# Attention by half-head tiles with the v transposes behind the first scores; an opening with latent x first and stationary conditioning weights

## The chip, the cores and the metric

One core of one Trainium2 chip. Its engines work side by side, each on its own queue in order: TensorE (PE; PEld is its weight load), VectorE (DVE), ScalarE (ACT), GpSimd (POOL) and SyncE (SP, which here issues most DMAs). The metric is the device time of one execution in microseconds; lower is better.

## The reference

Two layers over 512 latent and 256 context tokens of width 1024. Cut to what matters here:

```python
mod_lat = silu(c) @ ada_w[l] + ada_b[l]          # 6 x 1024 columns: shift, scale, gate, twice
mod_ctx = silu(c_ctx) @ ada_w[l] + ada_b[l]
h_lat = rmsnorm(x, norm1_g[l]) * (1 + sc1) + sh1
h_ctx = rmsnorm(ctx, norm1_g[l]) * (1 + csc1) + csh1
z = h @ w_in[l]                                  # branches A, B (q, k, v), C and gates
# branch B, for each of 8 heads, two halves a of 64 columns:
s = einsum('qad,kad->aqk', q, k) * 64 ** -0.5    # q and k normalised and rotated before
p = softmax(s)
out = (p[0] - lam * p[1]) @ v                    # latent queries see all 768 keys, context queries 256
```

Behind it stand the merge of the three branches, `w_out`, a residual, a second modulated norm and a gated feed-forward with a width-3 convolution. In layer 1 only keys and values of the context are wanted.

## The kernel before, in words

Activations lie with features on the 128 partitions and tokens along the row. Products that must be accurate are done in three passes: each operand is split into a rounded high part (`hh`, `whi`; a cast on ACT) and a low part (`hl`, `wlo`; a subtraction on DVE), and high x high, low x high and high x low are added up in PSUM (`gemm`, L183 to L186). Weights come through `Stream`: raw tiles of 512 KB (`wraw`), two deep, cast by `split_to` and finished by `low`.

The order of every instruction is the order in which Python emits it. `weave` mixes generators: each yields an estimated cost, and the one that is least far along in its own total goes next. So the costs that are yielded, and the totals given beside them, are what sets the order on each engine.

The opening (`startup`, L413) loads x by feature tiles of all 768 tokens, and the conditioning weights in chunks of 512 columns, through one SP queue. The vector silu(c), silu(c_ctx) is the stationary operand of two columns, a raw weight row of 512 the moving one (`ada_pe`, L209, in plain fp32); a copy and four small transposes turn the row into columns. One chunk goes over DVE (`ada_dve`, L233). The squares of x are added up, a matmul with ones (L335) gives the sum per token, an inverse root follows in small DVE steps (`rsqrt_ops`), and a matmul (L349) spreads it over the partitions. Then x is normalised and modulated tile by tile (`norm_apply`, L360), and `step` (in `halves`) multiplies each ready tile with the first three weights of branch C.

Attention runs over the eight heads. While the scores and softmax of head h go on (`attn`), the projections of head h + 1 are woven in (`project`: products of 256 columns, L647 to L649, in pieces of 12; then v). Between two heads stands a turn (`turn`, L1333): `qk_tr` transposes rotated q and k in three token pieces and splits them into high and low parts. The tile `qk` holds for each half a of the head high and low parts in different partitions, `qw` the same for q with the two swapped, by DMA. A product of branch C (`c_fill`) fills PE meanwhile. `v_tr` then transposes and splits v. `attn` goes block by block over 128 queries: `scores` (L825) does the matmuls into PSUM (two buffers), a row minimum on DVE (`mn`), an exponential on ACT (`pa`); `combine` subtracts the two halves; `to_at` transposes the result and splits it (`ah`, `al`); `av` multiplies with v.

Of the kernel before, what the change touches and what calls it, by code (L numbers as in the profile page):

```python
# [11 lines left out]
F32 = mybir.dt.float32  # L12
# [117 lines left out]
class Net:  # L130
# [78 lines left out]
    def ada_pe(self, l, n):  # L209
        nc = self.nc  # L210
        ps = self.ad.tile([128, 512], F32, tag="ad", name="ad")
        for q in range(8):
            if q % 2 == 0:
                two = self.ast.take("k", l, n, q // 2)
            raw = two[:, q % 2 * 512:q % 2 * 512 + 512]
            nc.tensor.matmul(ps[0:2, :], lhsT=self.silu[:, q, :], rhs=raw, start=(q == 0), stop=(q == 7))
            if q % 2:
                self.ast.load_to(len(self.ast.keys) + self.ast.bufs)
            if q < 7:
                yield 1000  # L220
        rows = self.small.tile([2, 512], F32, tag="adarow", bufs=1, name="adarow")
        nc.scalar.copy(rows, ps[0:2, :])
        yield 1000

        def fin():
            pt = self.ad.tile([128, 512], F32, tag="ad", name="ad")
            for i in range(4):
                nc.tensor.transpose(pt[:, 2 * i:2 * i + 2], rows[:, i * 128:(i + 1) * 128], self.ident[0:2, 0:2])
            pv = pt[:, 0:8].rearrange("p (i s) -> p s i", s=2)
            self.ada_fin([pv[:, s, :] for s in range(2)], l, n)  # L230
        yield fin

    def ada_dve(self, l, n):  # L233
        nc = self.nc
        ns = 2 if l == 0 or n < 4 else 1
        acc = [self.ast.pool.tile([128, 512], F32, tag=f"aacc{s}", bufs=2, name="aacc") for s in range(ns)]
        for q in range(8):
            if q % 2 == 0:
                two = self.ast.take("k", l, n, q // 2)
            raw = two[:, q % 2 * 512:q % 2 * 512 + 512]  # L240
            for s in range(ns):
                sc = self.silu[:, q, s:s + 1]
                if q == 0:
                    nc.vector.tensor_scalar(acc[s], raw, sc, None, ALU.mult)
                else:
                    nc.vector.scalar_tensor_tensor(acc[s], raw, sc, acc[s], ALU.mult, ALU.add)
            if q % 2:
                self.ast.load_to(len(self.ast.keys) + self.ast.bufs)
            yield 1000

        def fin():
            pt = self.ad.tile([128, 512], F32, tag="ad", name="ad")
            for s in range(ns):
                for i in range(4):
                    nc.tensor.matmul(pt[:, 4 * s + i:4 * s + i + 1], lhsT=acc[s][:, i * 128:(i + 1) * 128],
                                     rhs=self.ones[:, 0:1], start=True, stop=True)
            self.ada_fin([pt[:, 4 * s:4 * s + 4] for s in range(ns)], l, n)
        yield fin
# [101 lines left out]
    def norm_apply(self, tmp, sc, xs, rb, seg, cut=8, pre=False):  # L360
# [52 lines left out]
    def startup(self, xp, xt, load_x, pkeys, evac):  # L413
        nc = self.nc
        pa, pb = self.parts()
        self.ast.start(xp, 2, 7, nc.sync)
        for n in (1, 1, 2, 1, 2, 1):
            for _ in range(n):
                load_x()
            self.ast.load_to(self.ast.loaded + (len(xt) > 1))  # L420
        self.ws.late = True
        rb = xp.tile([128, T], F32, tag="rb", bufs=1, name="rb")
        ada = self.ada_chunks(self.ada_pe, [(0, 2), (0, 0)])
        g3, g1 = (self.ada_chunks(f, [(0, n)]) for f, n in ((self.ada_dve, 3), (self.ada_pe, 1)))

        def two(*gs):
            for g in gs:
                next(g)
                next(g)

        k = 0
        for i in range(16):
            next(ada)
            if i == 2:
                self.ws.load_to(2)
            while k < 8 and i >= (1, 2, 4, 6, 8, 9, 10, 11)[k]:
                for o, m, _ in (pa, pb):
                    self.sq_acc(xp, k, xt[k][:, o:o + m], o, m)
                k += 1
            if i == 12:  # L440
                r = self.norm_stat(0, T)
            if i == 14:
                self.ws.split_to(1)
                self.ast.limit += 8
                self.ast.load_to(11)
                self.ws.load_to(3)
        self.ws.low()
        self.ws.split_to(2)
        self.norm_rows(rb[:, 0:512], r, 512)
        sc = self.scales(0, 0)  # L450
        self.scales_set(sc, 0, 0, 0, 4)
        self.norm_h()
        step, finish = self.halves(pkeys, self.segs, evac)
        tmp = lambda: xp.tile([128, T], F32, tag="nsq", bufs=2, name="nt")
        ga, gb = (self.norm_apply(tmp, sc, [x[:, o:o + m] for x in xt], rb[:, o:o + m], (o, m, s), 4, s == 0)
                  for o, m, s in (pa, pb))
        next(ga)
        for _ in ada:
            pass
        self.norm_rows(rb[:, 512:768], r[:, 4:6], 256)  # L460
        self.ast.load_to(15)
        for k in range(4):
            next(ga)
            if k in (0, 3):
                self.ws.low()
            step(k, pa, 0)
            if k:
                step(k - 1, pa, 1)
            if k == 1:
                self.ws.split_to(3)  # L470
        step(3, pa, 1)
        two(g3)
        two(g1)
        for k in range(4):
# [3 lines left out]
            if k:  # L478
                two(g3)
                if k == 3:  # L480
                    for _ in g3:
                        pass
                two(g1)
        step(0, pa, 2)
        step(1, pa, 2)
        for _ in g1:
            pass
        step(2, pa, 2)
        step(3, pa, 2)
        self.scales_set(sc, 0, 0, 4, 8)  # L490
        next(ga)
        for k in range(4, 8):
            step(k, pa, 0)
            step(k, pa, 1)
            next(ga if k < 7 else gb)
        for k in range(4, 8):
            if k < 7:
                next(gb)
            step(k, pa, 2)
# [1044 lines left out]
```

## Time and profile before

| | |
|---|---|
| median of three runs | 2684.49 us (2683.94 to 2686.37) |
| profiled execution | 2683.64 us, its span 2681.9 us |
| PE busy | 2611.5 us (97%) |
| DVE busy | 1660.8 us (62%) |
| ACT busy | 1011.5 us (38%) |
| POOL busy | 220.6 us (8%) |
| bytes moved | 254.33 MB, 95 GB/s over the span |

The span runs from the first to the last instruction; all times inside it count from its start. Busy shares hold for the whole span, while each stage has its own limit: the opening up to about 76 us, attention of layer 0 to about 556, of layer 1 from about 1600 to 2000, and between and after them merge and feed-forward. Matmuls are pipelined and their ends are modelled, so the distance between the starts of two of them is the cost of one, not the duration that the row shows.

### The profile page before, as it was taken

Reading aid. Unit: us, or ns where it says so; the run is one execution under the profiler, and the core shown is the slowest. Engines: PE = TensorE matmul, PEld = TensorE weight load, DVE = VectorE, ACT = ScalarE, POOL = GpSimd, SP = SyncE. Lnnn points to the kernel's source line nnn. Section 1 sums busy time; section 2 is a strip of 40 time slices with the busy share of each in tenths; the row PEclk is TensorE's granted clock in tenths of the full one; section 3 lists DMA queues with packets and bytes.
Section 4 is the critical chain, followed back from the end, with each engine's and each line's share of the span. In section 5 each row is a group of like instructions: output and inputs, shape, how many; then the busy total and the mean of one; then the engine's idle time right before and its main releaser. Section 6 shows DMA issues by size and latency. Waiting matters only on the chain.

```text
span 2681.9 us, 36899 instructions
## 1 busy us (share of the span) xinstructions
PE 2611.5 (97%) x14952; PEld 2254.3 (84%) x14952; DVE 1660.8 (62%) x2895; ACT 1011.5 (38%) x1711; POOL 220.6 (8%) x202
## 2 busy tenths in 40 slices
PE   8999999999999999999999999999999999999999
PEld 3889989888888888888888878888878888888887
DVE  5677877756556437544544567877867554654444
ACT  3455455442122224312322334554553232342432
POOL 0000000001111110100100100000001122020101
PEclk8999999999999999999999999999999999999999
DMA  5211221224233331222222232212125545233333
GB/s 224 81 44 58 57 69 48 58 73 146 96 126 105 108 134 63 79 79 79 79 79 79 85 104 67 67 51 65 56 69 171 175 164 180 71 95 102 94 103 110
DMA packets 79658, 254.33 MB, mean 95 GB/s; under 512 B 9200, under 2 KB 19712, under 8 KB 79104
## 3 DMA queue, kind: packets, MB, share of 16 engines
q1 hardware_dynamic: 64512, 196.64, 22.8%
q0 software_dynamic: 14544, 55.07, 6.4%
q8 instruction: 118, 1.93, 0.3%
q14 instruction: 52, 0.43, 0.0%
q10 hardware_dynamic: 432, 0.27, 0.0%
HBM read 234.63 MB, written 6.82 MB: 90 GB/s over the span
## 4 chain that ended last, share of the span: by engine, by line
PE 78%; DVE 14%; ACT 5%; issue 2%; DMA 1%; DVEq 0%; POOL 0%; SPq 0%; ACTq 0%; POOLq 0%
PE mm L183 22%; PE mm L186 21%; PE mm L184 21%; DVE wlo L69 3%; PE S L838 2%; ACT pa L847 2%; PE mm L647 2%; PE mm L648 2%; PE mm L649 2%; DVE qk L727 2%; ACT whi L83 1%; PE mmT L871 1%; DVE mn L845 1%; ACT qk L726 1%; DVE zs L697 1%
## 5 line engine op out<-in xcount | busy, mean ns | idle before, releaser
L183 PE MATMUL mm<-hh,whi 128*128 128x512 f32 (+1 forms) x2392 | 854.5, 357 | 11.9 <-ACT hh L376 9.8
L184 PE MATMUL mm<-hl,whi 128*128 128x512 f32 (+1 forms) x2392 | 819.1, 353 | 4.4 <-DVE hl L379 4.1
L186 PE MATMUL mm<-hh,wlo 128*128 128x512 f32 (+1 forms) x2392 | 752.2, 353 | 1.3 <-DVE wlo L69 1.3
L183 PEld LDWEIGHTS mm<-hh,whi 128*128 128x128 f32 x2392 | 452.2, 189 | 104.7 <-ACT hh L376 13.3
L184 PEld LDWEIGHTS mm<-hl,whi 128*128 128x128 f32 x2392 | 452.4, 189 | 69.0 <-DVE hl L379 9.3
L69 DVE TENSOR_TENSOR wlo<-wraw,whi 128x1024 fp32r<-128x1024 f32 x320 | 399.4, 1249 | 179.2 <-ACT whi L83 177.5
L186 PEld LDWEIGHTS mm<-hh,wlo 128*128 128x128 f32 x2392 | 414.3, 190 | 41.5 <-DVE wlo L69 3.5
L83 ACT CAST whi<-wraw 128x1024 fp32r<-128x1024 f32 x320 | 334.6, 1047 | 291.7 <-PE mm L184 250.1
L996 DVE SCALAR_TENSOR_TENSOR cv<-mm,pc,cv 128x511 f32<-128x511 f32 (+1 forms) x132 | 86.8, 658 | 181.8 <-ACT cv L995 180.9
L183 PE MATMUL mm<-ah,whi 128*128 128x512 f32 (+1 forms) x528 | 187.9, 356 | 0.0
L847 ACT ACTIVATE pa<-S,mn 128x768 f32<-128x768 f32 (+1 forms) x160 | 129.3, 813 | 150.1 <-DVE mn L845 122.6
L647 PE MATMUL mm<-whi,hh 128*128 128x256 f32 x640 | 183.3, 286 | 1.3 <-DVE cp L775 0.8
L648 PE MATMUL mm<-wlo,hh 128*128 128x256 f32 x640 | 181.1, 283 | 0.8 <-DVE wlo L69 0.8
L649 PE MATMUL mm<-whi,hl 128*128 128x256 f32 x640 | 180.9, 283 | 0.0
L184 PE MATMUL mm<-al,whi 128*128 128x512 f32 (+1 forms) x528 | 179.9, 354 | 0.0
L186 PE MATMUL mm<-ah,wlo 128*128 128x512 f32 (+1 forms) x528 | 161.7, 355 | 0.0
L995 ACT ACTIVATE cv<-mm,pc 128x512 f32<-128x512 f32 (+1 forms) x132 | 88.7, 705 | 177.2 <-PE mm L186 177.2
L1157 DVE SCALAR_TENSOR_TENSOR x<-mm,mod,x 128x512 f32<-128x512 f32 (+1 forms) x91 | 58.2, 659 | 138.7 <-PE mm L186 138.7
L1200 POOL TENSOR_TENSOR cv<-cv 128x768 f32<-128x768 f32 (+1 forms) x44 | 91.5, 2080 | 605.2 <-DVE cv L998 420.7
L647 PEld LDWEIGHTS mm<-whi,hh 128*128 128x128 f32 x640 | 121.7, 190 | 4.2 <-ACT cp L773 1.0
L648 PEld LDWEIGHTS mm<-wlo,hh 128*128 128x128 f32 x640 | 122.0, 191 | 1.3 <-DVE wlo L69 1.2
L649 PEld LDWEIGHTS mm<-whi,hl 128*128 128x128 f32 x640 | 121.9, 190 | 0.0
(232 smaller groups left out, 4028.4 us busy)
## 6 DMA issues: line engine op xcount, KB each, us to landing
wraw<-w SPq DMA_DIRECT2D x320, 512.0 KB, 3.6
araw<-ada POOLq DMA_DIRECT2D x80, 512.0 KB, 4.0
qw<-qk SPq DMA_DIRECT2D x80, 128.0 KB, 2.5
araw<-ada SPq DMA_DIRECT2D x16, 512.0 KB, 7.4
x<-xT SPq DMA_DIRECT2D x8, 384.0 KB, 6.1
srow<-sscr POOLq DMA_DIRECT2D x3, 1024.0 KB, 5.4
x<-xT POOLq DMA_DIRECT2D x8, 384.0 KB, 5.9
xscr<-x SPq DMA_DIRECT2D x8, 256.0 KB, 3.9
```

The source lines that it names most:

```text
L69: self.lo_eng.tensor_tensor(lo, raw, hi.bitcast(F32), ALU.subtract)
L83: self.nc.scalar.copy(hi, raw)
L183: nc.tensor.matmul(ps[:, :m], lhsT=hh, rhs=xh[:, o:o + m], start=st, stop=False)
L184: nc.tensor.matmul(ps[:, :m], lhsT=hh, rhs=xl[:, o:o + m], start=False, stop=False)
L186: nc.tensor.matmul(ps[:, :m], lhsT=hl, rhs=xh[:, o:o + m], start=False, stop=sp)
L647: nc.tensor.matmul(ps[:, :256], lhsT=hh[:, sl], rhs=hi[:, c:c + 256], start=(k == 0), stop=False)
L648: nc.tensor.matmul(ps[:, :256], lhsT=hh[:, sl], rhs=lo[:, c:c + 256], start=False, stop=False)
L649: nc.tensor.matmul(ps[:, :256], lhsT=hl[:, sl], rhs=hi[:, c:c + 256], start=False, stop=(k == 7))
L847: nc.scalar.activation(pa[:, :nk], ss[a], AF.Exp, bias=mn[:, a:a + 1], scale=-1.0, accum_out=sm[a])
L995: nc.scalar.activation(dst[:, o:o + m], s, AF.Identity, scale=w[1], bias=bias)
L996: nc.vector.scalar_tensor_tensor(dst[:, o + 1:o + m], s[:, :m - 1], w[0], dst[:, o + 1:o + m], ALU.mult, ALU.add)
L1200: nc.gpsimd.tensor_tensor(cs[1][:, :n], cs[1][:, :n], cs[0][:, :n], ALU.mult)
```

## The change

In attention: `qk` becomes two tiles, one for each half; both copies of a piece stand ahead of both subtractions; `qw` is filled by four DMAs a piece instead of two; `v_tr` moves out of the turn to behind the first block's scores; the costs of the interleaving are new, and the last head's total of filler with them. In the opening: the 512 latent tokens of x are loaded first and the 256 context tokens later; the four chunks of conditioning cover two feature tiles each (256 shift and 256 scale columns), their weights are the stationary operand in blocks of 128 columns and the two silu columns the moving one; `ada_pe`, `ada_dve` and their row copies are gone. The steps of branch C and the norms are put in a new order between the chunks.

```diff
-    def ada_pe(self, l, n):
...
-            nc.tensor.matmul(ps[0:2, :], lhsT=self.silu[:, q, :], rhs=raw, start=(q == 0), stop=(q == 7))
...
-    def ada_dve(self, l, n):
...
+    def ada_cols(self, l, j):
         nc = self.nc
         ps = self.ad.tile([128, 512], F32, tag="ad", name="ad")
+        for i in range(4):
+            two = self.ast.take("s", l, j, i)
+            for q in (2 * i, 2 * i + 1):
+                for c in range(4):
+                    c0 = q % 2 * 512 + c * 128
+                    nc.tensor.matmul(ps[:, 2 * c:2 * c + 2], lhsT=two[:, c0:c0 + 128], rhs=self.silu[:, q, :],
+                                     start=(q == 0 and c == 0), stop=(q == 7 and c == 3))
+            self.ast.load_to(len(self.ast.keys) + self.ast.bufs)
+            yield
+        pv = ps[:, 0:8].rearrange("p (t k s) -> p s t k", t=2, s=2)
+        cut = lambda a: a.rearrange("p (t k) -> p t k", t=2)[:, :, 2 * j:2 * j + 2]
+        for s in range(2):
+            nc.vector.tensor_tensor(cut(self.mod[l][s][:, 0:16]), pv[:, s], cut(self.pc[l][:, PC_ADAB:PC_ADAB + 16]), ALU.add)
...
-    def norm_apply(self, tmp, sc, xs, rb, seg, cut=8, pre=False):
+    def norm_apply(self, tmp, sc, xs, rb, seg, cut=(8,), pre=False):
...
-            t1 = scaled(k + 1) if k + 1 not in (cut, 8) else None
+            t1 = scaled(k + 1) if k + 1 not in cut else None
...
     def startup(...)
+        for k in range(8):
+            xt.append(xp.tile([128, T], F32, tag=f"x{k}", name="x"))
+            nc.sync.dma_start(xt[k][:, 0:512], self.d["xT"][k][:, 0:512])
         self.ws.late = True
+        self.ws.load_to(1)
+        self.ast.start(xp, 4, 8, nc.sync)
+        self.ast.load_to(4)
+        self.ws.load_to(2)
+        self.ast.load_to(8)
...
+        for k in range(8):
+            self.sq_acc(xp, k, xt[k][:, 0:512], 0, 512)
+        self.ws.split_to(1)
+        ra = self.norm_stat(0, 512)
+        self.ws.load_to(3)
         self.ws.low()
+        for k in range(8):
+            nc.sync.dma_start(xt[k][:, 512:768], self.d["xT"][k][:, 512:768])
...
+        cut = (2, 4, 6, 8)
+        ga = self.norm_apply(tmp, sc, [x[:, 0:512] for x in xt], rb[:, 0:512], pa, cut, True)
+        gb = self.norm_apply(tmpc, sc, [x[:, 512:768] for x in xt], rb[:, 512:768], pb, cut)
+        def cond(j):
+            yield from self.ada_cols(0, j)
+            self.scales_set(sc, 0, 0, 2 * j, 2 * j + 2)
+        c = cond(0)
+        for _ in range(3):
+            next(c)
+        self.norm_rows(rb[:, 0:512], ra, 512)
+        for _ in c:
+            pass
         next(ga)
+        for k in (0, 1):
+            next(ga)
+            step(k, pa, 0)
+            step(k, pa, 1)
+        for _ in cond(1):
             pass
+        for k in (0, 1):
+            step(k, pa, 2)
+        for k in (2, 3):
             next(ga)
+            for i in range(3):
+                step(k, pa, i)
+        for k in range(8):
+            self.sq_acc(xp, k, xt[k][:, 512:768], 512, 256)
+        r = self.norm_stat(512, 256, True)
+        for _ in cond(2):
+            pass
+        self.tick(99)
+        self.norm_rows(rb[:, 512:768], r, 256)
         for k in range(4):
             next(gb)
             for i in range(3):
                 step(k, pb, i)
+        for _ in cond(3):
             pass
         for k in range(4, 8):
+            next(ga)
+            for i in range(3):
+                step(k, pa, i)
+            next(gb)
...
     def qk_tr(self, l, h, pool, st):
-        qk = pool.tile([128, 2, 2, T], F32R, tag="qk", bufs=1, name="qk")
+        qk = [pool.tile([128, 2, T], F32R, tag=f"qk{a}", bufs=1, name="qk") for a in range(2)]
...
-            for i, j in ((0, 64), (64, 0)):
-                hi = qk[i:i + 64, q0:, i // 64, t]
-                nc.scalar.copy(hi, pv[i:i + 64, q0:])
-                nc.vector.tensor_tensor(qk[j:j + 64, q0:, i // 64, t], pv[i:i + 64, q0:], hi.bitcast(F32), ALU.subtract)
+            his = [qk[a][64 * a:64 * a + 64, q0:, t] for a in range(2)]
+            for a in range(2):
+                nc.scalar.copy(his[a], pv[64 * a:64 * a + 64, q0:])
+            for a in range(2):
+                j = 64 - 64 * a
+                nc.vector.tensor_tensor(qk[a][j:j + 64, q0:, t], pv[64 * a:64 * a + 64, q0:], his[a].bitcast(F32), ALU.subtract)
             if q0 == 0:
-                for i, j in ((0, 64), (64, 0)):
-                    nc.sync.dma_start(qw[i:i + 64, :, t].bitcast(F32), qk[j:j + 64, 0, :, t].bitcast(F32))
-            yield 2200
+                for a in range(2):
+                    for i, j in ((0, 64), (64, 0)):
+                        nc.sync.dma_start(qw[i:i + 64, a, t].bitcast(F32), qk[a][j:j + 64, 0, t].bitcast(F32))
+            yield 1300
...
     def attn(self, l, h, pool, st):
+            if i == 0:
+                for c in self.v_tr(l, h, pool, st):
+                    yield c
+                    left -= c
             yield left
...
-        return [1500] * 4 + [2500] * 4 if l else [2000] * 10
+        return [3200] + [2200] * 3 + [1800] * 4 if l else [3200] + [2000] * 9
...
-                        run(self.v_tr(l, h, ap, st[h]))
...
-                            weave(a, (fill(99), (1 + N_VS) * (6000 if l else 10000)), tick=tick)
+                            weave(a, (fill(99), (1 + N_VS) * 10.4 * (512 if l else 768)), tick=tick)
```

## Rows read from the trace of the kernel before

**Rows 1.** Stretches: busy time of PE, PEld, DVE, ACT, POOL; clock; DMA share; GB/s.

```profile
76.00:556.00 480.00, 460.84 (x3191) 421.11 (x3190) 354.78 (x683) 243.14 (x519) 1.07 (x2) 1.00 0.21 60
```

**Rows 2.** Waits of PEld, 76 to 556: engine, line, releaser: total us, times, longest.

```profile
PEld S L838 <- ACT pa L847: 15.9, 30, 1.4
PEld mmT L883 <- ACT ah L875: 4.3, 2, 3.5
PEld S L838 <- DVE qk L727: 4.2, 9, 0.7
PEld mmT L759 <- DVE cc L799: 3.0, 3, 1.0
```

**Rows 3.** Waits of PEld, 1610 to 2000.

```profile
PEld S L838 <- ACT pa L847: 17.4, 32, 1.6
PEld S L838 <- DVE qk L727: 5.9, 8, 1.6
PEld mmT L759 <- issue: 1.6, 1, 1.6
```

**Rows 4.** Timeline, DVE and PE, 232 to 236: start, duration, engine, line, operation [idle before].

```profile
232.88 1.02 DVE L762 TENSOR_TENSOR vl<-mmT,vh 128x512 fp32r<-128x512 f32 x2
...
233.82 1.81 DVE L845 TENSOR_REDUCE mn<-S 128x1 f32<-128x768 f32 x2
...
235.85 0.61 PE L838 MATMUL S<-qk 128*128 128x512 f32 x2 [0.88 <-ACT pa L847]
```

**Rows 5.** Line L727: who waited for it, us in total and times.

```profile
  ACT qk L726: 89.0, 48
```

**Rows 6.** Timeline of the opening, PE and DVE.

```profile
24.76 1.47 PE L335 MATMUL st<-ones,nacc 128*128 128x1 f32 x12 [0.66 <-DVE nacc L324]
...
26.47 0.17 DVE L152 TENSOR_SCALAR rsy<-nv 128x6 int32<-128x6 int32 x1
...
28.48 0.17 DVE L163 SCALAR_TENSOR_TENSOR rsy<-rst,rsy 128x6 f32<-128x6 f32 x1
...
62.91 0.51 PE L183 MATMUL mm<-hh,whi 128*128 128x512 f32 x1 [0.35 <-ACT hh L376]
...
76.13 0.28 PE L186 MATMUL mm<-hh,wlo 128*128 128x256 f32 x1
```

**Rows 7.** Timeline, PE: weight loads of 128 columns for one moving column.

```profile
55.41 1.84 PE L255 MATMUL ad<-ones,aacc 128*128 128x1 f32 x16
```

**Rows 8.** Timeline, DVE, layer 1: the start of two ropes.

```profile
1678.62 0.68 DVE L697 TENSOR_TENSOR zs<-zs,rsy 128x512 f32<-128x512 f32 x1
...
1681.34 0.68 DVE L697 TENSOR_TENSOR zs<-zs,rsy 128x512 f32<-128x512 f32 x1
```

**Rows 9.** Timeline, SP's DMA queue, layer 1: two copies issued.

```profile
1871.97 1.32 SPq L730 DMA_DIRECT2D qw<-qk  x2
```

**Rows 10.** The page's DMA issues: count, KB each, median us to landing.

```profile
qw<-qk SPq DMA_DIRECT2D x80, 128.0 KB, 2.5
```

**Rows 11.** Stretches of the opening, columns as in rows 1.

```profile
20.00:27.00 7.00, 6.04 (x26) 2.29 (x25) 4.12 (x14) 3.78 (x7) 0.00 (x0) 0.97 1.03 409
27.00:30.00 3.00, 3.00 (x4) 0.38 (x3) 2.66 (x12) 0.00 (x0) 0.00 (x0) 0.51 1.03 410
54.00:58.00 4.00, 4.00 (x28) 3.10 (x28) 1.23 (x4) 0.00 (x0) 0.00 (x0) 1.00 0.00 0
```

**Rows 12.** Timeline, PEld, the last head of layer 0: starts and durations.

```profile
533.35 0.33 PEld L883 LDWEIGHTS mmT<-ah,vh 128*128 128x128 f32 x1
533.56 0.33 PEld L884 LDWEIGHTS mmT<-al,vh 128*128 128x128 f32 x1
...
535.33 0.19 PEld L884 LDWEIGHTS mmT<-al,vh 128*128 128x128 f32 x1
```

**Rows 13.** The chain that ended last, in order of time: start, us on the chain, what.

```profile
40.22 0.43 PE mm L183
59.73 0.23 PE mm L186
61.02 0.23 DVE mod L206 x2
```

More of the change, by code (lines that the diff above doesn't have):

```diff
@@ L207, in ada_fin @@
                                          self.pc[l][:, PC_ADAB + 4 * n:PC_ADAB + 4 * n + 4], ALU.add)
-    def ada_pe(self, l, n):
+    def ada_cols(self, l, j):
         nc = self.nc
         ps = self.ad.tile([128, 512], F32, tag="ad", name="ad")
[L212 to L215, printed above, removed]
-            nc.tensor.matmul(ps[0:2, :], lhsT=self.silu[:, q, :], rhs=raw, start=(q == 0), stop=(q == 7))
[L217 to L231, printed above, removed]
@@ L233, in ada_dve @@
-    def ada_dve(self, l, n):
[L234 to L258, printed above, removed]
@@ L411, in halves, with startup @@
         return step, finish
-    def startup(self, xp, xt, load_x, pkeys, evac):
+    def startup(self, xp, xt, pkeys, evac):
         nc = self.nc
         pa, pb = self.parts()
[L416 to L420, printed above, removed]
-        self.ws.late = True
-        rb = xp.tile([128, T], F32, tag="rb", bufs=1, name="rb")
[L423 to L446, printed above, removed]
@@ new lines, in startup @@
+        for k in range(8):
+            xt.append(xp.tile([128, T], F32, tag=f"x{k}", name="x"))
+            nc.sync.dma_start(xt[k][:, 0:512], self.d["xT"][k][:, 0:512])
+        self.ws.late = True
+        self.ws.load_to(1)
[3 more added lines that the diff above has]
+        self.ast.load_to(8)
+        rb = xp.tile([128, T], F32, tag="rb", bufs=1, name="rb")
+        tmp = lambda: xp.tile([128, T], F32, tag="nsq", bufs=2, name="nt")
@@ L447, in startup @@
+        tmpc = lambda: xp.tile([128, 256], F32, tag="nsc", bufs=2, name="nt")
+        for k in range(8):
[3 more added lines that the diff above has]
+        self.ws.load_to(3)
         self.ws.low()
-        self.ws.split_to(2)
-        self.norm_rows(rb[:, 0:512], r, 512)
+        for k in range(8):
+            nc.sync.dma_start(xt[k][:, 512:768], self.d["xT"][k][:, 512:768])
         sc = self.scales(0, 0)
-        self.scales_set(sc, 0, 0, 0, 4)
@@ L463, in startup @@
+        for _ in cond(1):
+            pass
+        for k in (0, 1):
+            step(k, pa, 2)
+        for k in (2, 3):
             next(ga)
[L464 to L473, printed above, removed]
+            for i in range(3):
+                step(k, pa, i)
+        for k in range(8):
+            self.sq_acc(xp, k, xt[k][:, 512:768], 512, 256)
@@ L477, in startup @@
                 step(k, pb, i)
[L478 to L486, printed above, removed]
-            pass
[L488 to L491, printed above, removed]
+        for _ in cond(3):
+            pass
         for k in range(4, 8):
[L493 to L499, printed above, removed]
+            next(ga)
+            for i in range(3):
+                step(k, pa, i)
+            next(gb)
         self.ws.low()
@@ L837, in scores @@
                     m = min(512, nk - o)
-                    nc.tensor.matmul(s[:, c0 + o:c0 + o + m], lhsT=(st["qw"][:, a] if v else st["qk"][:, 0, a])[:, t0:t0 + 128],
-                                     rhs=st["qk"][:, 1, a, k0 + o:k0 + o + m], start=(v == 0), stop=(v == 1))
+                    nc.tensor.matmul(s[:, c0 + o:c0 + o + m], lhsT=(st["qw"][:, a] if v else st["qk"][a][:, 0])[:, t0:t0 + 128],
+                                     rhs=st["qk"][a][:, 1, k0 + o:k0 + o + m], start=(v == 0), stop=(v == 1))
             ss.append(s[:, c0:c0 + nk])
```

18 lines of the change are left out of this document (4 added, 14 removed).

## The prediction

> **What bounds the kernel now.** I read the stretches first. In layer 0's attention TensorE (PE) is busy for 461 of 480 us at full clock, so what can be won there is PE's idle time and nothing else [rows 1]; layer 1's looks the same. Then the waits of PE's weight loads, which say what each idle stretch waited for. In layer 0's attention the scores matmuls waited 15.9 us for the exponentials (`pa`), 4.2 us for the split of q and k (`qk`), the v transposes 3.0 us for a PSUM buffer, and the last head's product with v 4.3 us for `ah` [rows 2]. In layer 1 the first two are 17.4 and 5.9 us, and the first head's v transposes waited 1.6 us [rows 3]. PE is in order, so such a wait is lost whole. Then the timeline of one change of head, for why the exponentials are late: VectorE (DVE) does `vl` (1.02 us) ahead of the row minimum `mn` at 233.82, and the scores of the second block wait at 235.85 for the exponential that needs that minimum [rows 4]. Last, who waited for L727: ScalarE (ACT) stood 89.0 us in 48 waits, one per q/k piece, because the second half's copy waits for the first half's subtraction [rows 5].
>
> The opening is another matter: PE runs through it until 76.25 (the last product of branch C starts at 76.13) [rows 6], and what stands there is order and clock.
>
> **Attention, layer 0.** Two edits act together. With one tile per half and both copies ahead of both subtractions, ACT no longer alternates with DVE, so the six subtractions of a turn follow each other, some 2 to 3 us sooner. With the v transposes behind the first scores, `vl` no longer stands ahead of `mn`, another 1.0 us. So `mn` is some 3 us sooner. Moreover the new cost 3200 of the first step makes the interleaving emit three pieces of the next head's projection before the second scores instead of two; with the transposes that is 3 x 1.44 + 0.8 = 5.1 us of PE work (12 products of 256 columns, 0.12 us apart as in rows 7, make a piece), against a chain minimum, exponential of 2 us. The scores' waits for `pa` go: -15.9. Of the 7.2 us for `qk` and `cc`, which fall mostly on three heads, 0.7 us a head stays, since their convolution still fills DVE: -5. That is -21. In the last head the lower total (23962 instead of 30000) spreads the filler: three quarter products of 0.7 us come behind the place where they were before, so the wait of 4.3 us loses about 2.5, and the fall of the clock behind it (some 16 products, 0.1 us each too slow [rows 12]) goes, 1.5: -4. Bounds: -29 (all waits of rows 2 and the clock) and -10 (of the `pa` waits only those of the second block, about 1.3 us in eight heads).
>
> **Attention, layer 1.** The `pa` waits go by the same argument (four pieces before the second scores): -17.4. But two new waits come. The order of emission, worked out by hand from the costs, puts the rope of the first token pair ahead of the last block's transposes; DVE then does 2.7 us of rope [rows 8] before `al` of that block, while only three pieces of 0.7 us lie between on PE instead of four with 3.5 us. Worked through, `al` comes 1.5 us late in seven heads: +10.5. And the scores start about 1 us earlier while q's swapped copy is now four transfers per piece instead of two, issued one behind the other by SP at 0.66 us [rows 9] and landing after 2.5 us [rows 10]: about 0.8 us of wait in eight heads, +6.5, in place of the waits of 5.9 for `qk` and 1.6 for the v transposes. Together -17.4 - 7.5 + 17 = -8. Bounds: -25 (no new wait) and +9 (each twice as dear). The weight loads queued behind the new transfers on SP start 2.6 us later at most; they have two projection halves of time, so that costs nothing.
>
> Attention: -21 - 4 - 8 = **-33 us**.
>
> **The opening.** Conditioning changes from 24 products of 512 columns with a two-column stationary, and one chunk on DVE, to 128 matmuls whose 128x128 weights are loaded for two columns each. The nearest row is L255, the same load for one column: 16 records for 8 matmuls in 1.84 us, 0.118 us a record [rows 7]. Four chunks of 64 records are 4 x 7.5 = 30 us of PE work. What they replace is inside the 76.25.
>
> At which clock? The stretch 20 to 27 shows a clock of 0.97 and 27 to 30 shows 0.51, half of 2.4 GHz [rows 11]: it fell at about 26.6 and rose again at 29.9. PE was busy for 6.04 of the 7 us before, and the last long thing that it did were the weight loads of L335, 1.47 us from 24.76 [rows 6]. I take it that the clock falls in each chunk as it fell there. What a record costs there: no row has loads alone at that level. The `av` products are 0.21 us apart with their loads lasting 0.33 us, against 0.19 us at full clock [rows 12]. Between 0.118 and 0.213 I take 0.213, as the load itself lengthens.
>
> The sum. Latent x (2.1 MB at 410 GB/s [rows 11]) and the last square and add: I estimate that PE starts at 11.5 (5.1 us of transfer, some 3 us of start and issue, and 3 us until the last sum is there), at the lower level. Statistic, first chunk and the row broadcast: 8 + 64 + 8 records x 0.213 = 17.0, so 28.5; modulation, scale, normalisation to the first product 2.5 (1.9 from 61.02 to 62.91 [rows 6, 13], plus the scale): 31. Products: 72 of 512 columns at 0.23 [rows 13] and 72 of 256 at 0.12, 25.2. Four blocks of them begin at the lower level; the low stretch of rows 11 lasted 3.3 us, and half of it is lost each time: 6.8. Three more chunks, each with 30 records at full clock before it falls and 34 at 0.213: 3.5 + 7.2 = 10.7, 32. Open gaps, PE in order: 1.0 after the second chunk; after the third the context's inverse root, which is now issued behind that chunk's modulation on DVE, 2.2 us from 26.47 to 28.65 [rows 6], with modulation and scale 0.5 before and broadcast, copy, scale and cast 2.0 behind, 4.7, and its statistic 0.5; after the fourth 2.3. Together 8.5. End: 31 + 25.2 + 6.8 + 32 + 8.5 = 103.5 against 76.25: **+27**. Bounds: +5 (full clock) and +42 (below). The context's x, moved behind the third weight on SP, which waits for the first low part, is wanted only after the second chunk; the weights and the later chunks land ahead of PE, which takes 1.9 us or more a tile against 1.3 of transfer. Both cost nothing.
>
> **Sum:** -33 + 27 = -6. The profiled execution took 2683.64 us, 0.85 under the median of 2684.49: 2677.6 profiled, **2678** as a median.
>
> **The rivals.** (a) The chunks cost no more than at full clock, because it does not fall in them or because the load does not depend on it. For: at 54 to 58, with 1.84 us of L255 in it, the clock stayed at 1.00 [rows 7, 11]. Against: 0.33 against 0.19 us. Then the opening is 25 + 25.2 + 3 x 7.5 + 8.5 = 81 to 88 (with or without the low blocks), +5 to +12, and the time 2684.5 - 33 + 9 = 2660. The Trainium skill, page "TensorE: Matmul & The Clock Gate", section "LDWEIGHTS (loading the stationary operand)", gives a load as its columns over 1.2 ns without naming the clock, some 107 ns for 128; by that a chunk would take the same time at either level. The trace's 0.33 us against 0.19 speaks against it.
>
> (b) The other side: the clock stays low through all of the opening up to the last block. All four chunks take 13.7, the 36 wide products before the last block 0.427 [rows 13], the 36 narrow ones 0.213: 31 + 41 + 15.4 + 7.7 + 14.3 + 8.5 = 118, +42, net +9: 2693. It decides from an end of the opening past 109; slower by over 0.2% from 115. For: the blocks between the chunks are only 3 to 8 us long. Against: the low stretch of rows 11 ended after 3.3 us, that of rows 12 by 535.33, where a load takes 0.19 us again.
>
> (c) Layer 1 gives nothing, its new waits eating all, and attention gives -25, the whole +2: 2687. For: `al` and the copies are late by the same DVE queue. Against: the waits that go are certain.
>
> (d) The tiles do not free ACT, since both engines read one PSUM tile: the alternation would then stand. The new order of the copies would still give most of it; it takes 3 us from the forecast and sits in its range.
>
> **Chances.** Forecast 0.42 (own range 2666 to 2690), (a) 0.27, (b) 0.15, (c) 0.12, better than all 0.04. About 0.2%, 5.4 us, is what can be told from no change. Faster: 0.25 of the forecast's, all of (a), 0.04: 0.57. Same: 0.14 + 0.09 of (c) + 0.02: 0.25. Slower: 0.03 + 0.03 + 0.12: 0.18. The range reaches to (a) and (b): 2652 to 2695.
>
> **What would show it.** The scores' waits for `pa` under 3 us in either layer, L726 no longer waiting for L727. New waits of L883 or L884 for `al` in layer 1, of the scores for `qw`. In the opening a granted clock near 0.5 in the second half of each chunk and records 0.21 us apart; the first projection product (77.22 now) near 104. At about 82 (a) holds; if the `pa` waits remain, the attention part is wrong.

## The result, and the profile after

| | before | after |
|---|---|---|
| median | 2684.98 us (2683.94 to 2686.37, 4 runs) | 2729.39 us (2726.38 to 2731.57, 4 runs) |
| profiled span | 2681.9 us | 2725.7 us |
| mean granted clock | 0.994 | 0.983 |

The ratio is 1.0164 [1.0148, 1.018]: the change made the kernel 44 us slower; 2678 with a range of 2652 to 2695 was forecast. To see where, four rows of TensorE's timeline cut each trace into stages: the first q/k projection product and the last product with v, in either layer. First the kernel before, then the one after; the first column is the start in us.

```profile
77.22 0.36 PE L647 MATMUL mm<-whi,hh 128*128 128x256 f32 x1 [0.81 <-DVE cp L775]
537.94 0.28 PE L885 MATMUL mmT<-ah,vl 128*128 128x256 f32 x1
1603.89 0.38 PE L647 MATMUL mm<-whi,hh 128*128 128x256 f32 x1 [0.51 <-ACT xb L351]
1994.62 0.28 PE L885 MATMUL mmT<-ah,vl 128*128 128x256 f32 x1
```
```profile
106.71 0.36 PE L597 MATMUL mm<-whi,hh 128*128 128x256 f32 x1 [0.81 <-DVE cp L728]
583.72 0.28 PE L838 MATMUL mmT<-ah,vl 128*128 128x256 f32 x1
1648.27 0.39 PE L597 MATMUL mm<-whi,hh 128*128 128x256 f32 x1 [0.51 <-ACT xb L317]
2038.09 0.28 PE L838 MATMUL mmT<-ah,vl 128*128 128x256 f32 x1
```

The same four rows were read from every kernel that ran; all differences between stages below come from this table (us). A stage is that of the one profiled execution, the last column the median of all:

| kernel | opening | attention, layer 0 | between | attention, layer 1 | median |
|---|---|---|---|---|---|
| before | 77.2 | 460.7 | 1066.0 | 390.7 | 2684.98 |
| after | 106.7 | 477.0 | 1064.5 | 389.8 | 2729.39 |
| attention part alone | 77.5 | 472.0 | 1068.0 | 390.4 | 2700.38 |
| opening part alone | 107.9 | 461.4 | 1067.8 | 390.3 | 2718.10 |
| after, piece behind | 107.7 | 442.1 | 1068.8 | 392.2 | 2700.57 |
| before, piece ahead | 77.5 | 483.3 | 1067.8 | 390.5 | 2708.43 |
| after, cast earlier | 107.2 | 454.1 | 1067.8 | 392.1 | 2710.02 |
| after, chunks woven | 119.0 | 474.5 | 1068.1 | 389.0 | 2741.72 |
| after, 128 columns | 92.2 | 471.7 | 1067.8 | 389.0 | 2715.79 |
| after, half the loads | 81.8 | 474.5 | 1067.8 | 388.1 | 2701.05 |
| combined, first | 78.0 | 443.4 | 1067.8 | 385.2 | 2663.25 |
| combined, GpSimd | 78.1 | 443.8 | 1066.6 | 387.5 | 2667.83 |
| combined, last | 77.3 | 442.1 | 1067.5 | 381.6 | 2659.07 |

So the opening lost 29.5 us (27 forecast), layer 1 won 0.9 (8 forecast), and layer 0's attention lost 16.3 where 25 were to be won. That one stage is 41 of the 51 us between forecast and measurement.

**Layer 0's attention after.** The waits of TensorE's weight loads, 107 to 584, answer to [rows 2] (the lists give total us, times, longest):

```profile
PEld mmT L836 <- ACT ah L828: 15.6, 9, 2.0
PEld mmT L837 <- DVE al L829: 13.1, 8, 1.8
PEld S L791 <- ACT pa L800: 1.9, 5, 0.6
```

The 15.9 us for `pa` went as forecast, but 28.7 us for `ah` and `al` came, most of it in one place of seven heads. That place in the first of them, timelines of PE, ACT and DVE (start, duration; in brackets the idle time before):

```profile
179.01 0.82 PE L824 MATMUL mmT<-ident,pa 128*128 128x128 f32 x6
...
182.82 0.39 PE L836 MATMUL mmT<-ah,vh 128*128 128x256 f32 x1 [1.60 <-ACT ah L828]
184.80 0.58 PE L837 MATMUL mmT<-al,vh 128*128 128x256 f32 x1 [1.59 <-DVE al L829]
```
```profile
180.32 1.04 ACT L83 CAST whi<-wraw 128x1024 fp32r<-128x1024 f32 x1
181.25 0.38 ACT L604 COPY zs<-mm 128x256 f32<-128x256 f32 x1
181.66 0.63 ACT L587 ACTIVATE sq<-zs 128x512 f32<-128x512 f32 x1
182.20 0.84 ACT L828 CAST ah<-mmT 128x512 fp32r<-128x512 f32 x2
```
```profile
182.33 0.69 DVE L588 TENSOR_REDUCE ss<-sq 128x8 f32<-128x512 f32 x1 [2.11 <-ACT sq L587]
182.93 1.22 DVE L69 TENSOR_TENSOR wlo<-wraw,whi 128x1024 fp32r<-128x1024 f32 x1
184.06 1.02 DVE L829 TENSOR_TENSOR al<-mmT,ah 128x512 fp32r<-128x512 f32 x2
```

The fourth block's transposes are done at 179.8, but ACT first does what came with the last projection piece: the next weight's cast, a copy and a square, and DVE a reduction and that weight's low part. TensorE has only one piece of v meanwhile and idles twice for 1.6 us. Then the clock falls, in all seven heads: over 181 to 189 the stretch reads 0.67 (columns as in rows 1).

```profile
181.00:189.00 8.00, 4.80 (x20) 4.31 (x20) 5.65 (x20) 2.18 (x6) 0.00 (x0) 0.67 0.22 68
```

Writing the order out from the costs shows why; what stands at the smaller share of its generator's total goes out first. Attention's total grew from 20000 to 21200 with the first step's 3200, and the fourth block's transposes moved from 0.600 of it (12000) to 0.623 (13200). The last q/k piece stands at 0.609 of the projection (14300 of 23500). So before, it went out behind the transposes; now it goes out ahead.

**Layer 1 after**, 1645 to 2039, answering to [rows 3]:

```profile
PEld mmT L837 <- DVE al L829: 9.1, 9, 1.2
PEld S L791 <- DMA qw<-qk: 6.5, 7, 1.1
PEld mmT L626 <- ACT kc L621: 5.9, 7, 0.8
PEld mmT L824 <- DVE al L829: 2.2, 7, 0.3
```

**The opening after**, TensorE's timeline, then stretches in the second chunk:

```profile
11.41 1.87 PE L301 MATMUL st<-ones,nacc 128*128 128x1 f32 x8 [11.41 <-DVE nacc L290]
14.56 10.37 PE L217 MATMUL ad<-silu,araw 128*128 128x2 f32 x48 [1.28 <-DMA araw<-ada]
32.12 0.79 PE L183 MATMUL mm<-hh,whi 128*128 128x512 f32 x1 [2.06 <-ACT hh L342]
...
57.41 10.65 PE L217 MATMUL ad<-silu,araw 128*128 128x2 f32 x64
...
105.62 0.28 PE L186 MATMUL mm<-hh,wlo 128*128 128x256 f32 x1
```
```profile
39.40:40.40 1.00, 1.00 (x11) 1.00 (x10) 0.00 (x0) 0.00 (x0) 0.00 (x0) 1.00 0.14 33
45.40:46.40 1.00, 1.00 (x6) 1.00 (x6) 0.00 (x0) 0.00 (x0) 0.00 (x0) 0.50 0.47 115
```

A chunk starts with eleven records in a microsecond at clock 1.00 and ends with six at 0.50 (those that reach over an edge of the stretch are counted). Up to about 40 us, where this trace first shows a change of the clock, the column reads 1.00, but the pace in the first chunk is that of 0.50: 48 records in 10.37 us are 0.216 us each.

### The profile page after: what moved, and what is told of

Read it like the earlier page. It is cut to its first block, busy times and chain, and to the rows that moved or that the text cites. A ratio compares the mean times of both kernels' runs of the same rounds, so it can differ in the third digit from the quotient of the medians.

```text
span 2725.7 us, 37500 instructions
## 1 busy us (share of the span) xinstructions
PE 2639.2 (97%) x15132; PEld 2310.8 (85%) x15132; DVE 1652.4 (61%) x2896; ACT 1010.7 (37%) x1708; POOL 220.5 (8%) x202
## 3 DMA queue, kind: packets, MB, share of 16 engines
q1 hardware_dynamic: 66944, 196.64, 22.9%
## 4 chain that ended last, share of the span: by engine, by line
PE 85%; DVE 7%; ACT 4%; DMA 2%; issue 1%; SPq 0%; POOL 0%; ACTq 0%; DVEq 0%; POOLq 0%
PE mm L183 23%; PE mm L186 22%; PE mm L184 22%; PE S L791 3%; PE mm L597 2%; PE mm L598 2%; PE mm L599 2%; PE ad L217 2%; DVE wlo L69 1%; DVE al L829 1%; PE mmT L837 1%; ACT pa L800 1%; ACT whi L83 1%; PE mmT L838 1%; DMA qw<-qk 1%
## 5 line engine op out<-in xcount | busy, mean ns | idle before, releaser
L183 PE MATMUL mm<-hh,whi 128*128 128x512 f32 (+1 forms) x2392 | 860.6, 360 | 15.6 <-ACT hh L342 13.6
```

The source lines that it names most:

```text
L183: nc.tensor.matmul(ps[:, :m], lhsT=hh, rhs=xh[:, o:o + m], start=st, stop=False)
```

## The experiments

**Does the moved piece make the loss?** In the kernel after, costs inside the projection put that one piece, with its cast and copies, behind the transposes again; the rest of the order stays.

```diff
                 if k == 3:
-                    yield 1300
+                    yield 1700 if l == 0 and b == 5 else 1300
...
-            yield 1300
+            yield 900 if l == 0 and b == 5 else 1300
```

> The kernel after, with one thing changed: in layer 0's attention the last piece of the next head's q/k projection (12 products of 256 columns, 1.44 us of TensorE) goes out behind the fourth block's transposes instead of ahead of them, as in the kernel before; with it go, on ScalarE, the cast of the next weight and the piece's copy and square, and on VectorE that weight's low part and a reduction. Theory (the order): the waits for ah and al in layer 0 (15.6 and 13.1 us) and the low clock behind each, some 2.5 us in seven heads, come from that one place; they fall under 4 us together, the low stretches of attention vanish, layer 0's stage goes from 477 to about 437 us, the time to 2689 us (2684 to 2697). Rival (load: the earlier scores and the v transposes crowd VectorE and ScalarE, wherever the piece stands): the waits stay over 20 us and the time at 2722 to 2730. Rival (the wait goes, but the low clock comes from elsewhere): about 2705.

Measured: 2700.57 us. Layer 0's attention takes 442.1 instead of 477.0, its clock reads 1.00 from 120 to 500, and 108 to 550 shows these waits:

```profile
PEld mmT L824 <- DVE al L829: 3.9, 7, 0.6
PEld mmT L836 <- DVE al L829: 2.5, 7, 0.4
```

The low clock and most of the waits are gone, as the theory says, but 8.2 us of waits for `ah` and `al` are left instead of under 4, and the stage is 5 us longer than expected. The total is some 4 us above its bound, since the stages that the edit does not touch are 1 to 4 us longer in this trace too. The load rival falls by the waits. The rival of a low clock from elsewhere falls by the clock column; the time alone, nearer to 2705 than to 2689, would not tell.

**Is the piece enough by itself?** The same swap the other way, in the kernel before.

```diff
-                    yield 1300
+                    yield 1000 if l == 0 and b == 5 else 1300
...
-            yield 1300
+            yield 1600 if l == 0 and b == 5 else 1300
```

> The kernel before, with the same swap the other way round: in layer 0's attention the last piece of the next head's projection goes out ahead of the fourth block's transposes. Nothing else of the change is in it. Theory (the order): seven heads get 1.6 + 1.6 us of waits for ah and al and a low clock behind them worth some 2.5 us each, so about +35 us and 2720 us (2710 to 2728), the waits for pa staying at 16 us. Rival (load): without the earlier scores and the moved v transposes the swap costs little, 2685 to 2692.

Measured: 2708.43 us (2703.83 to 2714.43). The waits for `ah` and `al` came almost whole, 25.2 us (78 to 561):

```profile
PEld S L838 <- ACT pa L847: 14.3, 30, 1.4
PEld mmT L884 <- DVE al L876: 13.0, 8, 1.8
PEld mmT L883 <- ACT ah L875: 12.2, 9, 3.5
```

The stage grew by 22.6 us, not 35, and the time is just under the expected range. TensorE's idle time in the stage grew by 12.4 us and its busy time, for the same 3087 records, by 10.2: the clock fell in four of the seven heads only, 0.98 over 120 to 500 against 0.96 in the kernel after. The four executions lie 10.6 us apart, with granted clocks from 0.988 (the longest) to 0.992 (the shortest). The cause holds; both shares were put too high.

**Do the parts add up?** The kernel before with the change's attention, and with its opening.

```diff
-        qk = pool.tile([128, 2, 2, T], F32R, tag="qk", bufs=1, name="qk")
+        qk = [pool.tile([128, 2, T], F32R, tag=f"qk{a}", bufs=1, name="qk") for a in range(2)]
...
+            if i == 0:
+                for c in self.v_tr(l, h, pool, st):
...
-        return [1500] * 4 + [2500] * 4 if l else [2000] * 10
+        return [3200] + [2200] * 3 + [1800] * 4 if l else [3200] + [2000] * 9
```

> The attention part of the change alone, on the opening of the kernel before. Theory: the parts add up. The stages of the two traces differ by +16.4 us in layer 0's attention, -0.8 in layer 1's and -1.3 in the rest: 2699 us (2696 to 2702). Rival: the low clock in layer 0's attention is an after-effect of the opening's; then it is gone here and the time is 2680 to 2686.

```diff
-            self.startup(xp, xt, load_x, ckeys(0), lambda key, pss: self.c_first(key, pss, S_FULL))
+            self.startup(xp, xt, ckeys(0), lambda key, pss: self.c_first(key, pss, S_FULL))
```

> The opening part of the change alone, with the attention of the kernel before. Theory: the parts add up, the first projection product starts 29.5 us later and nothing after it changes: 2714.5 us (2712 to 2717). Rival: part of the opening's time is found again in layer 0's attention (weights already there), 2705 or less.

Measured: 2700.38 and 2718.10 us, beside a kernel before of 2686.82 in that session: +13.6 and +31.3, together 44.9 us against 44.4 for the whole change. The second is 1 us above its range. The parts add up: with the old opening the clock of layer 0's attention is as low (0.96 over 120 to 500), and behind the new one the old attention takes what it took (461.4).

**Queue or cover?** In the kernel after, the next weight's cast goes out two pieces earlier; TensorE's order stays.

```diff
-            if b == 5:
+            if b == (5 if l else 4):
                 self.ws.ahead()
```

> The kernel after, with one thing moved: in layer 0's attention the next weight's cast (ScalarE, 1.04 us) and so its low part (VectorE, 1.22 us) go out one q/k piece pair earlier; TensorE's order, with the last piece ahead of the fourth block's transposes, is untouched. It splits the price of the swapped piece. Theory (queue): the casts stand behind the weight on ScalarE and VectorE; without it ah comes 1.0 us and al 2.0 us sooner in seven heads, the waits for ah and al fall from 28.7 to about 15 us, some low stretches go too, 2705 to 2715 us. Rival (cover): what counts is only that 1.44 us of TensorE work are missing between the transposes and the product; then the waits stay near 28 and the time near 2728.

Measured: 2710.02 us; layer 0's attention 454.1, 22.9 less than after. The waits, 108 to 561:

```profile
PEld mmT L824 <- ACT zs L604: 8.4, 7, 1.2
PEld mmT L836 <- ACT ah L828: 8.4, 9, 1.0
PEld mmT L837 <- DVE al L829: 5.1, 8, 0.7
```

Those for `ah` and `al` fell to 13.5 as expected, but a new one of 8.4 came, where the cast now stands ahead of a copy that frees a PSUM buffer. The stretches of the whole stage, of the kernel after, of this one and of after with the piece behind, split the gain, since TensorE does the same 3087 records in each:

```profile
106.71:583.72 477.01, 452.31 (x3087) 418.68 (x3088) 347.97 (x673) 229.41 (x500) 0.00 (x0) 0.96 0.20 58
```
```profile
107.24:561.36 454.12, 437.79 (x3087) 403.62 (x3088) 348.29 (x673) 229.06 (x500) 0.00 (x0) 1.00 0.21 61
```
```profile
107.65:549.76 442.11, 436.64 (x3087) 403.26 (x3088) 347.48 (x673) 229.53 (x500) 0.00 (x0) 1.00 0.22 63
```

Against after, this kernel idles 8.4 us less (24.7 and 16.3) and is busy for 14.5 us less, which I put down to the clock: it now stays up (1.00 against 0.96). With the piece behind the two are 19.2 and 15.7.

Many waits of up to 1.2 us left the clock alone here, while two of 1.6 us, 0.4 us apart, brought it down in all seven heads of the kernel after. They do not always: with the attention part alone the same pair, at 208.96 to 212.54, left it up in one head of seven. There:

```profile
212.00:216.00 4.00, 3.46 (x23) 3.23 (x24) 3.58 (x18) 0.37 (x1) 0.00 (x0) 1.00 0.42 131
```

So it was both queue and cover: of the 34.9 us between after and the piece behind, moving the casts alone wins 22.9, and the other 12.0 go with the piece itself.

**The opening: does breaking the chunks up keep the clock?** In the kernel after, each quarter of a chunk (16 records) goes between products.

```diff
-        for _ in cond(1):
-            pass
+        c = cond(1)
...
+            for i in range(2):
+                step(k, pa, i)
+                next(c)
...
```

> The kernel after, with the opening's second to fourth conditioning chunks dealt out a quarter at a time between the products of branch C, as far as the data allow; the same instructions, in another order on TensorE. Theory: TensorE's clock falls because a chunk is a stretch of weight loads with two moving columns each; broken into quarters of 16 records between products of 512 or 256 columns the granted clock stays at 1.00 for most of it and a record costs 0.12 us instead of 0.22, so that the first projection product starts at 90 to 97 instead of 106.7 and the time is 2712 to 2720. Rival: the records cost what they cost wherever they stand, or the waits for modulation and statistic set the opening; then it starts at 104 or later, 2727 or more.

Measured: 2741.72 us, the opening 119.0: worse than after. The rival's bound holds, but a record that costs the same wherever it stands doesn't explain 12 us more. TensorE's timeline:

```profile
33.82 3.41 PE L217 MATMUL ad<-silu,araw 128*128 128x2 f32 x16
37.09 0.77 PE L183 MATMUL mm<-hh,whi 128*128 128x512 f32 x1
37.66 0.63 PE L184 MATMUL mm<-hl,whi 128*128 128x512 f32 x1
38.09 0.63 PE L186 MATMUL mm<-hh,wlo 128*128 128x512 f32 x1
38.51 3.41 PE L217 MATMUL ad<-silu,araw 128*128 128x2 f32 x16
```

Sixteen records take 3.41 us, 0.213 each, and wide products stand 0.43 us apart: the low pace, in every quarter up to 68 us, and after a short rise the clock column reads 0.50 from 80 to 104. A few products between the loads did not lift the clock; they ran at its low level themselves. The theory as I put it fell.

**What does the low clock hang on?** The same loads, with 128 columns moved by each instead of 2.

```diff
-                    nc.tensor.matmul(ps[:, 2 * c:2 * c + 2], lhsT=two[:, c0:c0 + 128], rhs=self.silu[:, q, :],
+                    nc.tensor.matmul(ps[:, 128 * c:128 * c + 128], lhsT=two[:, c0:c0 + 128], rhs=self.silu[:, q, :].unsqueeze(1).to_broadcast([128, 64, 2]),
...
```

> The kernel after, with one thing changed in the opening: each of the 128 conditioning matmuls moves its two columns 64 times over (128 columns instead of 2; the result is the same columns, the other copies are not read). Same loads, same order, same places in TensorE's queue, more work a load. The woven order has just shown that breaking the chunks up does not bring the clock back (119 us, records 0.213 us apart until 70 us), so the question is what the low clock hangs on. Theory (thin work): the clock falls because of loads with hardly a column moved; with 128 columns the granted clock stays up, a matmul costs about 0.29 us (the 8 records of L349 in the kernel before: 1.16 us), a chunk 9.3 us at worst and all products run at full speed: first projection product at 85 to 95, time 2706 to 2718. Rival (a load's own price): the loads cost 0.21 us a record and the clock is as low as before, the added columns come on top or hide under the loads: 106 to 125, 2728 or more.

Measured: 2715.79 us, the opening 92.2, 14.5 less than after, with 64 times the columns. The second chunk's row of the timeline, then a stretch inside it:

```profile
32.15 7.30 PE L217 MATMUL ad<-silu,araw 128*128 128x128 f32 x64
```
```profile
34.00:39.00 5.00, 5.00 (x47) 5.00 (x47) 0.00 (x0) 0.00 (x0) 0.00 (x0) 1.00 0.90 279
```

The chunk takes 7.30 us instead of 10.92 and its clock stays at 1.00. A record costs 0.114 us with 128 columns, no more than with 2 at the same clock (a quarter of the woven order ran at the high pace, 16 in 1.84 us). The clock still falls where TensorE idles in this opening, behind the wait for the context's statistic:

```profile
57.00:66.00 9.00, 6.35 (x31) 5.85 (x32) 4.25 (x14) 2.19 (x5) 0.00 (x0) 0.62 0.00 0
```

So the low clock comes with loads that move hardly a column, and doing away with it in the chunks was worth 14.5 us of the opening. The trace is that of the shortest of four executions, 6 us under the other three; by the medians the kernel won 13.6.

**And the records themselves?** Half of the conditioning matmuls left out, everything around them kept.

```diff
-                for c in range(4):
+                for c in range(4) if q % 2 == 0 else ():
...
```

> The kernel after, with half of the conditioning matmuls left out (every second of the eight feature tiles of silu is not added in, so the modulation is another one); all loads from memory, waits and the order stay. Theory: the opening's loss is the chunks' records, 256 of them at 0.12 to 0.22 us on TensorE's path: 128 fewer take off 18 to 26 us, first projection product at 81 to 89, time 2702 to 2712. Rival: the opening is set by what surrounds the chunks (the weights' arrival, the statistic, the modulation): under 10 us come off, 2720 or more.

Measured: 2701.05 us, 1 us under its range, the opening 81.8, 24.9 less: 128 records at 0.19 us. What surrounds the chunks is not the bound.

**A version without the faults.** The opening of before, the change's attention, the piece behind, and three edits against layer 1's waits.

```diff
-            self.ws.ahead()
...
             nc.scalar.copy(kc, ps[:, :256])
+            self.ws.ahead()
...
-                    for i, j in ((0, 64), (64, 0)):
+                    for i, j in ((64 - 64 * a, 64 * a), (64 * a, 64 - 64 * a)):
...
-        return [3200] + [2200] * 3 + [1800] * 4 if l else [3200] + [2000] * 9
+        return [3200] + [2200] * 3 + [1800] * 3 + [2100] if l else [3200] + [2000] * 9
```

> The attention part alone on the opening of before, with the last piece behind the transposes in layer 0, and in layer 1 three edits against the three waits that were seen there: the copy of the context's keys ahead of the next weight's cast (kc, 5.9 us), the last cost 2100 instead of 1800, so that the last block's transposes come ahead of the first rope (al, 11.3 us), and of each pair of swapped copies of q the one of the high part first (qw, 6.5 us). Theory: layer 0's attention takes 442 us against 461, layer 1's 372 to 378 against 391 as each wait goes where its cause is taken away, and the time is 2652 us (2646 to 2660). Rival: in layer 1 VectorE is the bound behind these waits, each edit moves the wait to another place, layer 1 stays at 387 or more and the time at 2664 to 2670.

Measured: 2663.25 us, 0.9918 of before [0.9903, 0.9933]; layer 0's attention takes 443.4 as expected, layer 1's 385.2. That lies between theory (378) and rival (387), much nearer to the rival: `kc` is gone, but the other waits moved on (1588 to 1975).

```profile
PEld S L841 <- DMA qw<-qk: 11.2, 8, 1.7
PEld mm L183 <- DVE al L879: 5.7, 7, 0.8
```

**Is the queue the cause?** In that kernel the high part's copy goes through GpSimd's queue, and the costs bring the third block's transposes forward.

```diff
-                    for i, j in ((64 - 64 * a, 64 * a), (64 * a, 64 - 64 * a)):
-                        nc.sync.dma_start(qw[i:i + 64, a, t].bitcast(F32), qk[a][j:j + 64, 0, t].bitcast(F32))
+                    for e, i, j in ((nc.gpsimd, 64 - 64 * a, 64 * a), (nc.sync, 64 * a, 64 - 64 * a)):
+                        e.dma_start(qw[i:i + 64, a, t].bitcast(F32), qk[a][j:j + 64, 0, t].bitcast(F32))
...
+        return [3200] + [2300] * 3 + [1800] * 3 + [2400] if l else [3200] + [2000] * 9
```

> The kernel of the run before that was faster than both, with two further edits in layer 1's attention. There the scores' wait for qw had grown to 11.2 us: the copy of the high part stands on SyncE behind a weight load that waits for VectorE, although its data are there 2 us earlier; it now goes through GpSimd's queue, idle in this stage. And the costs are [3200] + [2300] x 3 + [1800] x 3 + [2400], by which the third block's transposes come ahead of the fourth piece of v, against the 5.7 us in which a product waited for a PSUM buffer until al was read. Theory: the queue is the cause; the waits for qw fall under 3 us, those for al under 2, layer 1 takes 370 to 375 us instead of 385, the time is 2650 us (2646 to 2656). Rival: the landing of the low part's copy, or GpSimd's slower queue, is late next: layer 1 stays at 380 or more, 2658 to 2666.

Measured: 2667.83 us, layer 1 387.5. The rival again: the scores still wait 11.3 us in eight heads, which the list puts down to "issue", and transposes of q and k another 5.7. At one turn (1755 to 1768) the copies landed this late (last number, median us from issue), those of the low part behind a weight load issued 0.7 us ahead of them:

```profile
wraw<-w SPq DMA_DIRECT2D x2, 512.0 KB, 4.5
qw<-qk POOLq DMA_DIRECT2D x4, 64.0 KB, 2.5
qw<-qk SPq DMA_DIRECT2D x4, 64.0 KB, 3.7
```

In the kernel before this one the median is 2.3 over all copies and 2.9 over layer 1's, so how much of the 3.7 is the load's is not shown.

**More work ahead of the wait.** Back on one queue, with another order of the first block's products:

```diff
+        for v, a in ((0, 0), (0, 1), (1, 0), (1, 1)) if first else ((0, 0), (1, 0), (0, 1), (1, 1)):
...
```

> The faster of the two kernels before (the one with all swapped copies on SyncE, 2663 us), with one change in TensorE's order: in the first block of each head both halves' products with the high part of q go ahead of the two products with the swapped copies, instead of half by half; 0.7 us more work ahead of the wait for qw. GpSimd's queue had only moved that wait (the low part's copy landed after 3.7 us instead of 2.3, beside a weight load). Theory: the copy's landing time is fixed by VectorE and SyncE, so the wait of 11.2 us in eight heads of layer 1 shrinks by 0.7 each to 5 to 7, layer 1 takes 379 to 381 us instead of 385 and the time is 2657 us (2654 to 2661). Rival: what is gained there is lost at the next wait of the head (minimum and exponential follow the same last product); layer 1 stays at 384 or more, 2662 to 2665.

Measured: 2659.07 us, **0.990 of before [0.9883, 0.9916]**, 27 us faster than it. Layer 1 takes 381.6, just above the expected 379 to 381; the wait for `qw` is 5.4 us with more work ahead of it:

```profile
PEld mm L183 <- DVE al L882: 5.7, 7, 0.8
PEld S L843 <- DMA qw<-qk: 5.4, 7, 1.4
```

## Why the prediction was wrong

- **Layer 0, the step that failed:** "the new cost 3200 of the first step makes the interleaving emit three pieces of the next head's projection before the second scores instead of two", and then "The scores' waits for `pa` go" and "That is -21". The waits went (15.9 to 1.9; `qk` and `cc` 7.2 to 0.3). But a piece taken forward is missing later, and I followed the order only up to the second scores. It was missing between the fourth block's transposes and their product, with its cast and copies now ahead of `ah` and `al`: 28.7 us of waits and some 15 us of low clock. Its bounds for this stage, -29 to -10, left it no way to lose; it lost 16.3. With the piece put back the stage gives -18.6, against -25 forecast; new waits for `al` are about the rest, 6 to 7 us. The sum also took more than there was: PE's idle time, "what can be won there", is 19 us by rows 1, while the waits of weight loads in rows 2 add up to 27.4, so not all of such a wait is time in which PE stands idle.
- **Layer 1:** of the terms, `pa` (17.4 to 0.9), `al` (+10.5 forecast, 11.3 measured) and `qw` (6.5 and 6.5) were right. Missing was `kc`, 5.9 us: the copy of the context's keys stands on ACT behind a weight's cast, and TensorE now has only a piece of v and a block of transposes to do until it wants it; before, a product with v lay there too. So -0.9, not -8, and rival (c) was nearer here.
- **ACT and the halves:** right. L726 waited 89.0 us for L727 [rows 5]; its successor L676 waits for no subtraction. Rival (d) falls.
- **The opening:** right in kind, and in size to some 2 us. Start 11.5 and 11.41, first product 31 and 32.12, a chunk 10.7 and 10.92, 10.65, 9.28, end 103.5 and 105.7. Two small errors partly cancel: the four blocks of products lost some 9 us to the low clock instead of 6.8, and the last chunk was shorter. That the clock falls after 30 records stood on no row; the clock column puts it after some 28, 32 and 45. The clock fell in each chunk as it had at [rows 11]. Rival (a) falls: within one chunk eleven records touch a microsecond at 1.00, six at 0.50. The Trainium skill ("TensorE: Matmul & The Clock Gate", "LDWEIGHTS (loading the stationary operand)") gives a load's time as its columns over 1.2 ns and names no clock; for 128 columns that is an estimate of 107 ns. The traces come near that at 1.00 (0.114 us a record in the run with 128 columns) and not at the low pace (0.213 in the woven order). Rival (b), 118, was not what the change did; the woven order came near it, 119.0, with a short rise at 70.
- **The sum:** -6 was right only if both halves were. The chance of slower, 0.18, came from the opening (rival (b)), from layer 1 (rival (c)) and from the spread of the forecast, none of it from layer 0 losing.
- **Slips in the working** that change little: a record at full clock is 0.115 us by rows 7 (1.84 over 16), not 0.118; the 0.12 us between products of 256 columns is not in rows 7, which show loads; four times half of 3.3 us is 6.6, not 6.8; the chances of faster add up to 0.56, those of rival (b) to 0.14 of 0.15.

## What to carry to other kernels

When a cost or a total in an interleaving changes, write out the whole order on every engine, not the part that the change is meant for: a piece that moves forward leaves a gap somewhere, and takes its copies and casts along to stand ahead of something else. Short idle stretches close together can cost a second time through the clock: in layer 0 some 15 us beside the 22 us of idling in those places. Weight loads with two moving columns were dear here, since TensorE fell to its low clock (0.50) in them; where the data must be stationary, moving more columns than needed can be the cheaper way, as it was in this opening (14.5 us).

## What was not expected of the hardware

- More work made a stretch shorter: 64 records with 128 columns took 7.30 us at clock 1.00, with 2 columns 10.92 us, most of it at 0.50.
- Products dealt out among such loads did not bring the clock up (16 records, three or six products of 512 columns, and so on from 34 to 68 us, all at the low pace); in the kernel after it rose during the unbroken runs of products.
- Two idle stretches of 1.6 us with one product between them brought the clock down in thirteen of the fourteen places where they occur in the kernel after and in the attention part alone, and left it up in one.
- What stays open: how much of the 29.5 us of the opening is the clock in all (some 14.5 by the run with 128 columns, in which it still fell twice), why the clock stayed up in that one head, why the copies of q land later in layer 1, and the 1 to 4 us by which untouched stages differ from one trace to the next.
